# Attention on one core: sixteen lifted VectorE groups in halves, sixteen DMA turns, and another order

## The chip, the cores and the metric

The kernel runs on one core of a Trainium2 chip. The metric is device time in microseconds (us). The core has TensorE for matmuls, ScalarE for activations, VectorE and GpSimd for elementwise work, and DMA engines that move data. Each engine works through its own queue of instructions in order; semaphores tie the queues together. Data come from HBM into SBUF; matmuls write to PSUM, which ScalarE and VectorE read.

## The reference: what is computed

Attention for 8 batches of 8 heads, with 512 positions of 64 columns, all in float32:

```
scores = einsum('bhqd,bhkd->bhqk', q, k) / sqrt(64)
attn   = exp(scores - scores.max(-1)) ; attn /= attn.sum(-1)
out    = einsum('bhqk,bhkd->bhqd', attn, v)
```

Two heads are a pair, so there are 32 pairs, 0 to 31. The inputs are 25.2 MB, the output 8.4 MB.

## The kernel before: tiling, stages and the written order

For a pair, `q`, `k` and `v` are loaded as three tiles of 256 KB (`load`, line 183, on SyncE's queue) and cast to fp16 by GpSimd (`cast`, 191). `q` and `k` then have to lie with the 64 columns on the partitions. For most pairs TensorE transposes them into PSUM (`transposes`, 238) and VectorE copies the result out (`copy`, 257); for the pairs in `BY_DMA` one DMA does both (`turn`, 250), issued from SyncE's queue between loads and stores.

The scores are worked in groups: 128 keys of both heads of a pair against 512 queries, so 128 partitions by 1024 columns of float32 in PSUM (`scores`, 274). There are three such buffers, `st0` to `st2`. The step `S12.0` computes group 12 into buffer 0. Four groups make a pair; pair g has the groups 4g to 4g+3, and the last group of pair 31 is split into two halves of its queries (steps 127 and 128). No maximum is subtracted; the sum of the exponentials comes from a column of ones beside `v`.

For most groups ScalarE then computes the exponential into an fp16 tile `pt` (line 306). For 14 groups, listed in `KIND`, VectorE does it instead. For those of kind C, F and S a further matmul with the constant `lift` (line 287) first puts a large number under the scores, so that the float's low 16 bits hold the fraction of the exponent, and the columns of `k` of that group are multiplied by 128 log2(e) when cast (line 210). Then VectorE makes the fp16 bits with a polynomial: `r` (`raise_`, 323) writes `z`, and `p12.0` to `p12.2` (`pass_`, 338) are the passes on all 1024 columns. Kinds C and F have four VectorE passes; S and X have three, and a middle step `m` on GpSimd (`middle`, 371: a `tensor_scalar` and a product). X is not lifted. The last pass of the lifted kinds reads two tiles in SBUF, `y` and `z`, and writes 32-bit words to a tile `pd`; the fp16 halves of these are what the next matmul reads.

The values follow: `V1.0.2.14.0` is pair 1, head 0, query block 2, unit 14, in PSUM bank `x0` (`values`, 424: four matmuls). Seven units share a bank; `R` (`invert`, 393) takes the reciprocals of their sums, `N` (`normalise`, 398) multiplies into a ring in SBUF, and `O` (`store`, 412) stores the next pair whose units are done, or one head if its second number is 0. The last head's values are in `L` (`last_values`, 449, in a score buffer) and `F` (`finish`, 466). `B` (`fill`, 439) are matmuls on constants.

Nothing is planned at run time: `ORDER` is a literal list of steps, and each engine gets its instructions in the order of that list. `lk8` loads, `ck8` casts; `cv1+p5.2` casts only after that VectorE step has finished. TensorE, too, works strictly in this order, so a score that waits for its buffer holds everything behind it.

Of the kernel before, what the change touches and what calls it, by code (L numbers as in the profile page):

```python
# [19 lines left out]
RAW, QK16, TQK, NV = 7, 6, 7, 12  # L20
# [16 lines left out]
V3.1.3.35.1 V4.0.0.36.1 V4.0.1.37.1 cq11 lk15 S32.2 ck11+cq1 N28.7 lk16 S33.0 V4.0.2.38.1 p30.0
T9.0.0 lk17 cq12 V4.0.3.39.1 T9.1.0 S34.2 cv6 lq16 V4.1.0.40.1 C9 V4.1.1.41.1 cq13 S35.0 lv13 R35.7
p30.1 T10.0.0 T10.1.0 lq17 S36.2 lk18 C10 S37.1 cv5+p30.1 S38.0 N35.7 ck12 T11.0.0 lv12 T11.1.0
p30.2 S39.2 V4.1.2.42.1 V4.1.3.43.1 V5.0.0.44.1 S40.1 C11 cv7+p30.1 ck13 r39 S41.0 lv14 T12.0.0 cv8  # L40
lq18 T12.1.0 S42.1 lk19 cv10 C12 V5.0.1.45.1 lq19 V5.0.2.46.1 ck14 V5.0.3.47.1 p39.0 V5.1.0.48.1
O21.1 S43.0 V5.1.1.49.0 O35.1 V5.1.2.50.0 V5.1.3.51.0 V6.0.0.52.0 lv15 S44.1 R42.7 ck15 p39.1
V6.0.1.53.0 lk20 ck16 S45.0 cq14+r39 lk21 V6.0.2.54.0 N42.7 S46.2 V6.0.3.55.0 p39.2 lv17 T13.0.1
T13.1.1 S47.1 lk22 R49.7 S48.0 C13 cv9+R49.7 O42.1 S49.2 r47 cv12 V6.1.0.56.1 V6.1.1.57.1
V6.1.2.58.1 cq15 V6.1.3.59.1 S50.0 N49.7 lv16 V7.0.0.60.1 ck17 V7.0.1.61.1 V7.0.2.62.1 p47.0 S51.2
lq20 V7.0.3.63.0 cv11 V7.1.0.64.0 V7.1.1.65.0 lq21 V7.1.2.66.0 S52.0 cq16 R56.7 N56.7 V7.1.3.67.0
lq22 V8.0.0.68.0 ck18+N49.7 p47.1 S53.2 lq23 V8.0.1.69.0 T14.0.1 cq17 T14.1.1 lk23 S54.0 R63.7 C14
S55.1 cq18+R63.7 lv19 N63.7 S56.2 T15.0.1 O49.1 p47.2 T15.1.1 V8.0.2.70.0 V8.0.3.71.0 lk24
V8.1.0.72.0 S57.0 C15 lq24 S58.1 V8.1.1.73.0 r57 V8.1.2.74.0 ck19+C15 T16.0.1 lk25 T16.1.1 S59.2
cq19 lv18 V8.1.3.75.0 C16 V9.0.0.76.0 cq20 S60.1 O56.1 R70.7 ck20 V9.0.1.77.1 N70.7 lq25 S61.2 p57.0  # L50
V9.0.2.78.1 V9.0.3.79.1 O63.1 T17.0.0 cq21+p47.2 T17.1.0 S62.1 cv13+C1 lk26 C17 S63.0 V9.1.0.80.1
V9.1.1.81.1 p57.1 lk27 V9.1.2.82.1 S64.2 V9.1.3.83.1 lq26 V10.0.0.84.0 V10.0.1.85.0 V10.0.2.86.0
R77.7 cv15+C17 V10.0.3.87.0 V10.1.0.88.0 N77.7 V10.1.1.89.0 lq27 V10.1.2.90.0 ck21+p57.0 S65.0 R84.7
S66.1 N84.7 T18.0.1 lk28 S67.2 p57.2 lv20 V10.1.3.91.0 T18.1.1 V11.0.0.92.0 lv22 S68.0 C18
ck22+p57.2 lq28 r68 S69.1 cq22+C18 T19.0.1 lk29 V11.0.1.93.0 cq23 V11.0.2.94.0 S70.2 O70.1 p68.0
ck23 V11.0.3.95.0 T19.1.1 V11.1.0.96.0 cq24 V11.1.1.97.0 S71.1 R91.7 S72.0 m68.0 N91.7 S73.2 u22 C19
S74.1 r72 T20.0.1 V11.1.2.98.0 T20.1.1 u23 V11.1.3.99.0 S75.2 C20 V12.0.0.100.0 V12.0.1.101.0 p72.0
S76.1 lk30 cv14 V12.0.2.102.0 V12.0.3.103.0 V12.1.0.104.0 V12.1.1.105.1 ck24 S77.2 lv21 R98.7 p72.1
V12.1.2.106.1 lq29 ck25 S78.1 u24 V12.1.3.107.1 N98.7 cq25 V13.0.0.108.1 V13.0.1.109.1 S79.0 p68.2
V13.0.2.110.1 T21.0.0 u25 T21.1.0 V13.0.3.111.1 S80.1 C21 ck26 S81.2 S82.0 cq26+r5 R105.7 lq30 r81  # L60
V13.1.0.112.0 V13.1.1.113.0 O77.1 V13.1.2.114.0 cq27 V13.1.3.115.0 V14.0.0.116.0 S83.1 lq31 cv16
V14.0.1.117.0 N105.7 V14.0.2.118.0 cq28 lv23 S84.0 p81.0 V14.0.3.119.1 cv17 lk31 V14.1.0.120.1
V14.1.1.121.1 V14.1.2.122.1 S85.1 cv19 R112.7 V14.1.3.123.1 N112.7 V15.0.0.124.1 ck27 V15.0.1.125.1
S86.0 lv24 R119.7 p81.1 V15.0.2.126.0 lv26 V15.0.3.127.0 V15.1.0.128.0 ck28 V15.1.1.129.0
V15.1.2.130.0 S87.1 cv18 N119.7 V15.1.3.131.0 V16.0.0.132.0 S88.2 cv21+R119.7 lv25 R126.7
V16.0.1.133.1 N126.7 V16.0.2.134.1 cq29 O91.1 V16.0.3.135.1 V16.1.0.136.1 V16.1.1.137.1 S89.0 u26
p72.2 V16.1.2.138.1 V16.1.3.139.1 V17.0.0.140.0 V17.0.1.141.0 S90.2 V17.0.2.142.0 R133.7 ck29 O98.1
V17.0.3.143.0 N133.7 V17.1.0.144.0 S91.1 u27 p81.2 V17.1.1.145.0 S92.0 S93.2 V17.1.2.146.0
V17.1.3.147.1 r93 V18.0.0.148.1 cv20+p81.2 lv28 V18.0.1.149.1 V18.0.2.150.1 S94.1 O105.1 cq30
V18.0.3.151.1 V18.1.0.152.1 R140.7 V18.1.1.153.1 ck30 u28 N140.7 S95.0 S96.2 cv22 R147.7  # L70
V18.1.2.154.0 N147.7 V18.1.3.155.0 cv23 V19.0.0.156.0 V19.0.1.157.0 O112.1 V19.0.2.158.0
V19.0.3.159.0 p93.0 lv27 S97.0 V19.1.0.160.0 V19.1.1.161.1 V19.1.2.162.1 V19.1.3.163.1 R154.7
cv25+C2 V20.0.0.164.1 S98.2 N154.7 S99.1 m93.0 u29 S100.0 r99 V20.0.1.165.1 V20.0.2.166.1
V20.0.3.167.1 V20.1.0.168.0 V20.1.1.169.0 lv29 S101.2 V20.1.2.170.0 R161.7 O119.1 V20.1.3.171.0
N161.7 V21.0.0.172.0 V21.0.1.173.0 S102.0 u30 p99.0 V21.0.2.174.0 V21.0.3.175.1 V21.1.0.176.1
V21.1.1.177.1 V21.1.2.178.1 cv24+r99 S103.2 R168.7 V21.1.3.179.1 O126.1 cv26+R161.7 N168.7
V22.0.0.180.1 V22.0.1.181.1 S104.1 O133.1 R175.7 m99.0 S105.0 N175.7 V22.0.2.182.0 O147.1
V22.0.3.183.0 V22.1.0.184.0 O154.1 V22.1.1.185.0 V22.1.2.186.0 p93.2 V22.1.3.187.0 S106.2 O161.1
V25.0.0.188.0 O161.0 S107.1 V25.0.1.189.1 R182.7 V25.0.2.190.1 lv30 N182.7 S108.0 V25.0.3.191.1 r108
V25.1.0.192.1 V25.1.1.193.1 V25.1.2.194.1 S109.2 V25.1.3.195.1 V23.0.0.196.0 V23.0.1.197.0 R189.7  # L80
V23.0.2.198.0 S110.0 N189.7 cq31 S111.1 p99.2 S112.2 V23.0.3.199.0 V23.1.0.200.0 V23.1.1.201.0
V23.1.2.202.0 V23.1.3.203.1 V26.0.0.204.1 ck31+r5 R196.7 S113.0 r111 V26.0.1.205.1 cv27+C2 u31
S114.2 cv28 V26.0.2.206.1 N196.7 V26.0.3.207.1 V24.0.0.208.1 V24.0.1.209.1 S115.0 O168.0 R203.7
V24.0.2.210.0 p108.0 V24.0.3.211.0 O175.1 V24.1.0.212.0 S116.2 O182.1 V24.1.1.213.0 V24.1.2.214.0
N203.7 lv31 V24.1.3.215.0 m108.0 S117.0 p111.0 O189.1 V26.1.0.216.0 V26.1.1.217.1 O203.1
V26.1.2.218.1 V26.1.3.219.1 B220.1 B220.1 V28.0.0.220.1 S118.2 O203.0 R210.7 V28.0.1.221.1 N210.7
V28.0.2.222.1 S119.0 p111.1 V28.0.3.223.1 O210.1 V28.1.0.224.0 V28.1.1.225.0 V28.1.2.226.0
V28.1.3.227.0 B228.1 B228.1 S120.2 cv29 R217.7 B228.1 B228.1 B228.1 B228.1 N217.7 B228.1 B228.1
B228.1 B228.1 B228.1 B228.1 B228.1 B228.1 S121.0 p108.2 S122.1 O217.0 B228.1 B228.1 B228.1 B228.1
V29.0.0.228.0 V29.0.1.229.0 V29.0.2.230.0 V29.0.3.231.1 V29.1.0.232.1 R224.7 V29.1.1.233.1 p111.2  # L90
V29.1.2.234.1 V29.1.3.235.1 S123.2 S124.0 N224.7 cv30+p108.2 S125.1 V27.0.0.236.1 cv31+R224.7 O224.1
V27.0.1.237.1 V27.0.2.238.0 V27.0.3.239.0 R231.7 V27.1.0.240.0 V27.1.1.241.0 N231.7 V27.1.2.242.0
V27.1.3.243.0 V30.0.0.244.0 S126.2 O231.1 R238.7 N238.7 S127.0 V30.0.1.245.1 V30.0.2.246.1 O238.1
# [7 lines left out]
def kernel(  # L101
# [29 lines left out]
    for m, kind in KIND.items():  # L131
        (g, c, _), (g2, c2, _) = groups[m]
        assert 0 < g == g2 < LAST and c == c2
        if kind in LIFTED:
            raises.setdefault(g, set()).add(c)
# [138 lines left out]
    def scores(m, b):  # L274
# [33 lines left out]
        )  # L308

# [331 lines left out]
```

## Time and profile before

| | |
|---|---|
| median of three runs | 116.86 us (117.65, 116.73, 116.86) |
| span of the profiled execution | 114.0 us |
| TensorE, VectorE, ScalarE, GpSimd busy | 104.0, 103.2, 107.2, 81.7 us |
| loads and stores, all queues | 36.44 MB, mean 320 GB/s |

One execution was profiled. Its span runs from the first to the last instruction; its own device time is not listed apart from the three runs, so the median stands beside it. In the profile's rows PE is TensorE, PEld its weight loads, DVE VectorE, ACT ScalarE, POOL GpSimd, SP SyncE; a q behind the name is the queue that issues DMAs. L306 is line 306 of the kernel. A row of a group gives busy us, the mean ns of one, and after the bar the idle time just before its instructions with what ended it. A row of the timeline gives start, duration, engine, line and what was done. A duration contains the latency to the end of the instruction, so that one instruction can start before the one ahead is done.

### The profile page before, as it was taken

How to read it: one execution, taken by the hardware profiler on the slowest of the kernel's cores; microseconds unless marked ns; L12 is line 12 of the kernel's file. 1: busy time of each engine (PE TensorE's matmuls, PEld its weight loads, DVE VectorE, ACT ScalarE, POOL GpSimd, SP SyncE). 2: the span in 40 equal slices, each digit the busy share in tenths (PEclk: the TensorE clock that was granted, in tenths of full speed). 3: DMA queues.
4: the chain of work that ended last, by engine and by line, in shares of the span. 5: the costliest groups of instructions: out<-in, count | busy, mean ns of one | idle time of the engine just before them, and what ended most of it. 6: DMA issues, size and time to landing. Idle time of an engine off the chain costs nothing.

```text
span 114.0 us, 3954 instructions
## 1 busy us (share of the span) xinstructions
PE 104.0 (91%) x1549; PEld 65.6 (58%) x1549; DVE 103.2 (91%) x178; ACT 107.2 (94%) x119; POOL 81.7 (72%) x126
## 2 busy tenths in 40 slices
PE   7968998999899898999998899999999999999980
PEld 5624554655464564655665456775657666676660
DVE  4557999999999999999999999999989999999761
ACT  4599999999999999999999999999999999999960
POOL 2369756298978967938849999996899999394300
PEclk9999999999999999999999999999999999999999
DMA  3999999999999999999999998989999699999665
GB/s 92 281 354 378 383 378 384 382 380 378 383 384 376 385 382 381 375 368 382 376 385 384 369 196 283 188 209 383 279 257 232 219 333 328 312 312 330 226 218 164
DMA packets 45619, 36.44 MB, mean 320 GB/s; under 512 B 12704, under 2 KB 45600, under 8 KB 45600
## 3 DMA queue, kind: packets, MB, share of 16 engines
q1 hardware_dynamic: 45168, 35.86, 102.2%
q10 hardware_dynamic: 432, 0.33, 0.9%
q8 instruction: 12, 0.20, 0.7%
q14 instruction: 7, 0.06, 0.1%
HBM read 25.17 MB, written 8.39 MB: 294 GB/s over the span
## 4 chain that ended last, share of the span: by engine, by line
DVE 34%; PE 29%; ACT 23%; issue 5%; DMA 4%; POOL 1%; SPq 1%; ACTq 0%
ACT pt L306 23%; PE o L431 14%; PE st L301 13%; DVE y L361 12%; DVE tqk L266 6%; DVE z L328 5%; DVE ring L404 4%; DVE pd L361 4%; DMA k<-in_k_dram 4%; DVE rc L396 1%; PE tp L246 1%; PE o L441 1%; SPq L486 1%; DVE tqk L260 1%; PE st L287 1%
## 5 line engine op out<-in xcount | busy, mean ns | idle before, releaser
L306 ACT ACTIVATE pt<-st 128x1024 f16<-128x1024 f32 (+1 forms) x112 | 102.3, 1097 | 0.4 <-PE st L301 0.4
L301 PE MATMUL st<-tqk 64*128 64x512 f16 (+1 forms) x250 | 46.7, 380 | 5.3 <-ACT pt L306 3.5
L431 PE MATMUL o<-vp,pt 128*128 128x65 f16 x912 | 45.4, 195 | 0.0
L431 PEld LDWEIGHTS <-pt 128*128 128x128 f16 x912 | 36.2, 98 | 14.5 <-issue 13.3
L195 POOL CAST vp<-v 128x512 f16<-128x512 f32 x32 | 24.1, 768 | 8.5 <-DVE pd L361 2.8
L301 PEld LDWEIGHTS <-tqk 64*128 64x128 f16 x250 | 14.2, 93 | 17.9 <-issue 7.8
L404 DVE TENSOR_TENSOR ring<-o,rc 128x448 f32<-128x448 f32 (+2 forms) x37 | 22.5, 608 | 1.0 <-DVE rc L396 0.2
L220 POOL CAST qkp<-k 128x512 f16<-128x512 f32 (+3 forms) x27 | 18.0, 672 | 4.7 <-issue 2.4
L220 POOL CAST qkp<-q 128x512 f16<-128x512 f32 x30 | 18.1, 611 | 1.6 <-DVE y L361 0.8
L328 DVE TENSOR_SCALAR z<-st 128x1024 f32<-128x1024 f32 x14 | 17.0, 1211 | 1.4 <-PE st L301 1.3
L361 DVE SCALAR_TENSOR_TENSOR pd<-y,z 128x1024 uint32<-128x1024 f32 x12 | 15.3, 1272 | 0.0
L431 PE MATMUL o<-vp,pd 128*128 128x65 f16 x96 | 15.1, 195 | 0.0
L246 PE MATMUL tp<-ident,qkp 128*128 128x128 f16 x168 | 14.6, 220 | 0.4 <-POOL qkp L220 0.2
L361 DVE SCALAR_TENSOR_TENSOR y<-st,z 128x1024 f32<-128x1024 uint16 x12 | 14.6, 1213 | 0.0
L266 DVE COPY tqk<-tp 128x1024 f16<-128x1024 f16 x20 | 13.6, 682 | 0.1
L246 PEld LDWEIGHTS <-qkp 128*128 128x128 f16 x168 | 9.8, 97 | 4.5 <-issue 1.6
L431 PEld LDWEIGHTS <-pd 128*128 128x128 f16 x96 | 9.4, 98 | 2.7 <-issue 2.2
L361 DVE SCALAR_TENSOR_TENSOR y<-st,y 128x1024 f32<-128x1024 uint16 x9 | 10.9, 1209 | 0.0
L396 DVE RECIPROCAL rc<-o 128x7 f32<-128x7 f32 (+2 forms) x37 | 7.2, 195 | 1.3 <-PE o L431 1.3
L208 POOL CAST qkp<-k 128x384 f16<-128x384 f32 (+2 forms) x8 | 3.3, 412 | 4.8 <-DVE pd L361 3.3
L210 POOL TENSOR_SCALAR qkp<-k 128x128 f16<-128x128 f32 x12 | 6.3, 527 | 0.2
L376 POOL TENSOR_SCALAR t<-y 128x1024 f32<-128x1024 f32 x4 | 4.2, 1045 | 2.4 <-DVE y L361 2.1
(58 smaller groups left out, 52.1 us busy)
## 6 DMA issues: line engine op xcount, KB each, us to landing
v<-in_v_dram SPq DMA_DIRECT2D x32, 256.0 KB, 5.4
k<-in_k_dram SPq DMA_DIRECT2D x31, 256.0 KB, 5.4
q<-in_q_dram SPq DMA_DIRECT2D x31, 256.0 KB, 5.4
out_dram<-ring SPq DMA_DIRECT2D x29, 256.0 KB, 4.8
out_dram<-ring SPq DMA_DIRECT2D x5, 128.0 KB, 3.1
k<-in_k_dram ACTq DMA_DIRECT2D x2, 128.0 KB, 2.8
q<-in_q_dram SPq DMA_DIRECT2D x2, 128.0 KB, 2.6
tqk<-qkp SPq DMA_TRANSPOSE x10, 5.3
```

The costliest lines, as they stand in the source:

```text
L195: return nc.gpsimd.tensor_copy(out=vps[g % NV][:, :, :, 0:D], in_=raw[g]["v"][:, :, :, :])
L210: nc.gpsimd.tensor_scalar(out=dst[:, :, c : c + 1], in0=src[:, :, c : c + 1], scalar1=128.0 * LOG2E, scalar2=None, op0=AluOp.mult,)
L220: parts.append(nc.gpsimd.tensor_copy(out=dst[:, :, a:NI], in_=src[:, :, a:NI]))
L246: nc.tensor.transpose(tps[g][:, n, i, :], qkp[g][:, n, i, :], ident)
L266: nc.vector.tensor_copy(out=tqk[g][:, :, :], in_=tps.pop(g).rearrange("p n i c -> p n (i c)"))
L301: nc.tensor.matmul(st[:, x, cols], kc, qc[:, cols], start=kind is None or kind not in LIFTED, stop=True)
L306: nc.scalar.activation(out=pt[:, :, cols], in_=st[:, :, cols], func=EXP, scale=scale)
L328: nc.vector.tensor_scalar(out=r["z"][:, :, :], in0=r["st"][:, :, :], scalar1=2.0**17 if lifted else 128.0 * LOG2E, scalar2=None if lifted ...
L361: nc.vector.scalar_tensor_tensor(out=r["bits"][:, :, :] if last else y, in0=(zero, one, y)[s], scalar=(QUARTIC if quartic else CUBIC)[s], ...
L396: dve(nc.vector.reciprocal(out=rcs[u][:, 0:n], in_=o[:, x : x + n, D : D + 1]))
L404: nc.vector.tensor_tensor(out=ring[:, u % NU : u % NU + n, :], in0=o[:, x : x + n, 0:D], in1=rc[:, 0:n].broadcast_to([P, n, D]), op=AluOp. ...
L431: nc.tensor.matmul(os[u // 7][:, u % 7, :], blocks[(g, c, h)][:, y * P : (y + 1) * P], vps[g % NV][:, h, c, :], start=(c == 0), stop=(c == ...
```

## The change

16 groups instead of 14 go to VectorE, all of one kind. Each is lifted, and `k` of the 15 pairs that have such a group is scaled as a whole when cast, in one `tensor_scalar` with two operations (the second a product with 1); ScalarE's scale undoes it for the pair's other groups. The polynomial is written as a product: VectorE forms (x + a) times a constant (`r`), then (x + b) times that (`p..0`), GpSimd squares the result (`m`), and VectorE adds score and square (`p..2`) and writes fp16 bits straight to a `pt` tile. Each of these is done in halves of 512 columns, one head each; `r5.1` is the half of head 1. `pd` goes, and `pt` has 40 buffers instead of 30. The pairs 16 to 31, instead of 22 to 31, are turned by DMA. The order is another one in whole: groups are no longer in sequence, the lifted groups always use buffer 2, and no cast waits for a VectorE step any more.

```diff
-KIND = {5: "C", 12: "C", 20: "C", 30: "C", 39: "C", 47: "C", 57: "F", 68: "S", 72: "C", 81: "C", 93: "X", 99: "S", 108: "X", 111: "C"}
-BY_DMA = (22, 23, 24, 25, 26, 27, 28, 29, 30, 31)
+BY_VECTOR = (5, 12, 21, 28, 31, 46, 53, 59, 69, 72, 79, 91, 94, 107, 111, 115)
+BY_DMA = (16, 17, 18, 19, 20, 21, 22, 23, 24, 25, 26, 27, 28, 29, 30, 31)
...
+        if name == "k" and g in scaled:
+            return nc.gpsimd.tensor_scalar(
+                out=dst,
+                in0=src[:, :, :, :],
+                scalar1=to_bits,
+                scalar2=1.0,
+                op0=AluOp.mult,
+                op1=AluOp.mult,
+            )
...
+            scale=scale / to_bits if grp[0][0] in scaled else scale,
```

The steps `r`, `p` and `m` of the changed kernel, whole:

```python
    def raise_(m, h):
        r = raised[m]
        if "t" not in r:
            r["t"] = wpool.tile([P, 2, S], FP32, tag="z", name=f"t_{m}")
        dve(
            nc.vector.tensor_scalar(
                out=r["t"][:, h],
                in0=fraction(r["st"])[:, h],
                scalar1=ROOTS[0],
                scalar2=Q2**0.5,
                op0=AluOp.add,
                op1=AluOp.mult,
            )
        )

    def pass_(m, s, h):
        r = raised[m]
        t = r["t"][:, h]
        if s == 0:
            dve(
                nc.vector.scalar_tensor_tensor(
                    out=t,
                    in0=fraction(r["st"])[:, h],
                    scalar=ROOTS[1],
                    in1=t,
                    op0=AluOp.add,
                    op1=AluOp.mult,
                )
            )
            return
        dve(
            nc.vector.scalar_tensor_tensor(
                out=r["bits"][:, h],
                in0=r["st"][:, h],
                scalar=BOTTOM,
                in1=r["y"][:, h],
                op0=AluOp.add,
                op1=AluOp.add,
            )
        )

    def square(m, h, engine):
        r = raised[m]
        if "y" not in r:
            r["y"] = wpool.tile([P, 2, S], FP32, tag="y", name=f"y_{m}")
        t = r["t"][:, h]
        return engine.tensor_tensor(out=r["y"][:, h], in0=t, in1=t, op=AluOp.mult)

    def middle(m, h):
        square(m, h, nc.gpsimd)
```

Two stretches of the new order that the prediction speaks of, a turn up to its pair's first score, and the end:

```
S78.1 V13.0.1.109.1 cq25 V13.0.2.110.1 r79.0 V13.0.3.111.1 V13.1.0.112.0 cq24 S70.0 lv19 p79.0.0
V13.1.1.113.0 V13.1.2.114.0 cv14 u24 S76.1 R105.7 V13.1.3.115.0 N105.7 cq29 V14.0.0.116.0
V14.0.1.117.0 V14.0.2.118.0 p79.0.1 m79.0 S88.0 V14.0.3.119.1 V14.1.0.120.1 R112.7 lk31 S85.1 N112.7
m79.1 V14.1.1.121.1 O63.1 V14.1.2.122.1 p79.2.0 V14.1.3.123.1 V15.0.0.124.1 lv21 V15.0.1.125.1 S87.0
R119.7 ck29 O35.1 p79.2.1 V15.0.2.126.0 O7.1 S77.1 N119.7 S91.2 u25 V15.0.3.127.0 r91.1 S99.0
...
V29.1.0.232.0 V29.1.1.233.0 V29.1.2.234.0 R224.7 S127.0 S128.2 N224.7 V29.1.3.235.0 cv31
V27.0.0.236.0 V27.0.1.237.0 S121.1 R231.7 cv30 V27.0.2.238.1 L0.0 L1.0 V27.0.3.239.1 L2.2 F0
V27.1.0.240.1 V27.1.1.241.1 L3.2 N231.7 V27.1.2.242.1 V27.1.3.243.1 S124.1 F1 O224.1 V30.0.0.244.1
V30.0.1.245.0 V30.0.2.246.0 O238.1 R238.7 V30.0.3.247.0 V30.1.0.248.0 N238.7 V30.1.1.249.0
V30.1.2.250.0 V30.1.3.251.0 O245.1 R245.7 V31.0.0.252.1 V31.0.1.253.1 N245.7 V31.0.2.254.1
V31.0.3.255.1 R252.4 O231.1 N252.4 O252.0
```

More of the change, by code (lines that the diff above doesn't have):

```diff
@@ L90 @@
[L90 to L93, printed above, removed]
-V30.0.3.247.1 V30.1.0.248.1 V30.1.1.249.1 V30.1.2.250.1 V30.1.3.251.1 V31.0.0.252.0 V31.0.1.253.0
-R245.7 V31.0.2.254.0 V31.0.3.255.0 N245.7 S128.2 L0.0 R252.4 L1.0 O245.1 L2.1 N252.4 O252.0 F0 L3.1
@@ L327, in raise_ @@
         dve(
             nc.vector.tensor_scalar(
-                out=r["z"][:, :, :],
-                in0=r["st"][:, :, :],
-                scalar1=2.0**17 if lifted else 128.0 * LOG2E,
-                scalar2=None if lifted else 143.0 * 1024,
-                op0=AluOp.max if lifted else AluOp.mult,
-                **({} if lifted else {"op1": AluOp.add}),
-            )
-        )
-    def pass_(m, s):
-        r, kind = raised[m], KIND[m]
-        if kind in ("X", "Q") and s == 2:
+                out=r["t"][:, h],
```

245 lines of the change are left out of this document (98 added, 147 removed).

## The prediction

> **What bounds the kernel now.** First the page's engine totals, then the groups by shape.
>
> ```profile
> span 114.0 us, 3954 instructions
> PE 104.0 (91%) x1549; PEld 65.6 (58%) x1549; DVE 103.2 (91%) x178; ACT 107.2 (94%) x119; POOL 81.7 (72%) x126
> ...
> L306 ACT ACTIVATE pt<-st 128x1024 f16<-128x1024 f32 x110 | 101.2, 1106 | 0.1
> ```
>
> Three engines stand above 90%, so totals don't decide. The group does: the 110 exponentials of full size on ScalarE waited 0.1 us in all, and 101.2/110 = 0.92 us is the step from one to the next. The timeline of ScalarE's two ends says the same:
>
> ```profile
> 7.81 6.73 ACT L306 ACTIVATE pt<-st 128x1024 f16<-128x1024 f32 x7
> ...
> 102.53 7.06 ACT L306 ACTIVATE pt<-st 128x1024 f16<-128x1024 f32 x8
> 109.97 0.60 ACT L306 ACTIVATE pt<-st 128x512 f16<-128x512 f32 x1 [0.37 <-PE st L301]
> ```
>
> It runs from 7.81 to 109.59 without a gap (110 x 0.92 and one half of about 0.5 make 101.7). **ScalarE is the bound.** VectorE, GpSimd and TensorE matter only if late. What follows the last exponential is the tail; timeline of TensorE, VectorE and the two issuing queues:
>
> ```profile
> 108.03 1.58 PE L431 MATMUL o<-vp,pt 128*128 128x65 f16 x44
> 109.54 0.39 PE L301 MATMUL st<-tqk 64*128 64x256 f16 x2
> ...
> 110.62 0.30 PE L457 MATMUL o_last<-vp,pt 128*128 128x65 f16 x4 [0.21 <-ACT pt L306]
> ...
> 109.92 0.17 DVE L396 RECIPROCAL rc<-o 128x4 f32<-128x4 f32 x1
> 110.13 0.42 DVE L404 TENSOR_TENSOR ring<-o,rc 128x256 f32<-128x256 f32 x1
> ...
> 110.58 0.34 SPq L422 DMA_DIRECT2D out_dram<-ring  x1
> 111.02 0.40 SPq L479 DMA_DIRECT2D out_dram<-obl  x1
> ...
> 111.48 0.35 ACTq L479 DMA_DIRECT2D out_dram<-obl  x1
> ...
> out_dram<-ring SPq DMA_DIRECT2D x5, 128.0 KB, 3.1
> ...
> out_dram<-obl SPq DMA_DIRECT2D x1, 64.0 KB, 2.0
> out_dram<-obl ACTq DMA_DIRECT2D x1, 64.0 KB, 1.7
> ```
>
> The last store (64 KB, issued at 111.48) lands 1.7 later, at 113.2; 0.8 us closes the span at 114.0. The tail after the last exponential (110.57) is 3.4 us. The span stands against runs of 116.73 to 117.65 (median 116.86): 2.9 us lie around it, and I carry them over.
>
> **ScalarE.** 16 lifted groups instead of 14 leave 108 full exponentials: 2 x 0.92 = **-1.84 us**, where every step stays dense. The changed scale factor of some costs nothing: same instruction, same size.
>
> **VectorE.** Its timeline:
>
> ```profile
> 19.55 0.68 DVE L266 COPY tqk<-tp 128x1024 f16<-128x1024 f16 x1
> 20.15 0.61 DVE L404 TENSOR_TENSOR ring<-o,rc 128x448 f32<-128x448 f32 x1
> 20.68 1.22 DVE L361 SCALAR_TENSOR_TENSOR pd<-y,z 128x1024 uint32<-128x1024 f32 x1
> 21.82 0.68 DVE L266 COPY tqk<-tp 128x1024 f16<-128x1024 f16 x1
> ```
>
> Start to start, 1024 columns cost 1.14 and 448 cost 0.53; the line through both gives 0.60 at 512, of which 0.06 is fixed. Out go 14 `r` and 38 `p` steps, 52 x 1.14 = 59.3; in come 16 groups x 3 passes x 2 halves, 96 x 0.60 = 57.6. Six pairs fewer are copied from PSUM (0.60 each, 19.55 to 20.15): -3.6. Sum -5.3 us, and it buys only slack, since ScalarE ends last. [...]
>
> **GpSimd.** Its timeline, then groups by shape.
>
> ```profile
> 5.99 0.29 POOL L208 CAST qkp<-k 128x128 f16<-128x128 f32 x1 [1.47 <-DMA k<-in_k_dram]
> ...
> 85.90 1.89 POOL L379 TENSOR_TENSOR y<-t 128x1024 f32<-128x1024 f32 x1
> 87.74 1.17 POOL L195 CAST vp<-v 128x512 f16<-128x512 f32 x2
> ...
> 62.97 1.04 POOL L376 TENSOR_SCALAR t<-y 128x1024 f32<-128x1024 f32 x1
> 64.10 2.36 POOL L379 TENSOR_TENSOR y<-t,y 128x1024 f32<-128x1024 f32 x1
> ...
> L220 POOL CAST qkp<-q 128x512 f16<-128x512 f32 x30 | 18.1, 611 | 1.6 <-DVE y L361 0.8 <-DVE rc L396 0.5 <-DMA q<-in_q_dram 0.3
> L210 POOL TENSOR_SCALAR qkp<-k 128x128 f16<-128x128 f32 x12 | 6.3, 527 | 0.2
> L208 POOL CAST qkp<-k 128x128 f16<-128x128 f32 x3 | 0.9, 292 | 1.5 <-DMA k<-in_k_dram 1.5
> ```
>
> A square of 1024 takes 1.84 start to start; a half lies between 0.92 and, with the casts' fixed 0.19, 1.04: I take 1.0, so 32 halves add 32 us, and four middle steps go (1.04 with 1.89 or 2.36, some 13 in all). Casts follow 0.56 us apart (two take 1.17). Fifteen `k` tiles are now scaled whole, a form not in the trace (512 columns, two operations, fp16 out). From below it is the plain cast, 0.61; from above it is the 128-column scaling, 0.527, stretched by four less its fixed part: (0.527 - 0.19) x 4 + 0.19 = 1.54. The two-operation row (1024 columns in 1.04) lies on the casts' line (0.19 + 0.83 per 1000 columns), so I take 0.61. Counted so along the order, GpSimd has 12 squares and 44 casts = 36.6 us ahead of the 48th score step, from its first cast at 5.99 to 42.6; ScalarE by then has 41 exponentials, 7.81 + 37.7 = 45.5. So GpSimd leads by **2.9 us** at most. About half goes at the start, when loads and the first square's input aren't there yet; 1.5 us is the slack I use. The passes with two SBUF inputs (`pd<-y,z`) are gone: each new pass reads one operand in PSUM. The waits that put casts behind those passes go too. I cost that at nothing gained, since ScalarE never waited for it. [...]
>
> **TensorE.** Chain of waits:
>
> ```profile
> 54.84 0.45 PE tp L246 x8
> ...
> 84.88 0.22 PE st L287 x2
> ```
>
> Six pairs of transposes go, 12 steps `T` of four matmuls each (eight in 0.45: -2.7). 16 groups are lifted where 12 were (the two of kind X had no lift): 4 x 0.22 = +0.9. Fill matmuls stay at 44. TensorE only has to stay ahead; nothing is gained from it.
>
> **DMA and its queue.** Six more pairs are turned by DMA. View of the tile `tqk`, then half-microsecond windows around one turn:
>
> ```profile
> L252 SPq DMA_TRANSPOSE tqk<-qkp x10: 1237/1720/3149, 62.0 to 97.7; - x10
> ...
> DMA to landing us min/median/max: 3.7/5.3/6.2
> ...
> 81.00:81.50 0.50, 0.50 (x13) 0.35 (x12) 0.50 (x2) 0.50 (x2) 0.50 (x2) 1.00 1.16 403
> 81.50:82.00 0.50, 0.50 (x11) 0.20 (x7) 0.47 (x2) 0.50 (x2) 0.50 (x2) 1.00 4.13 252
> 82.00:82.50 0.50, 0.50 (x12) 0.27 (x9) 0.47 (x3) 0.50 (x2) 0.50 (x2) 1.00 0.03 3
> ```
>
> A turn's 256 KB pass in about 0.9 us (126 KB in the second window, the rest in the first), so six cost the engines some 5 us, and hold the queue 6 x 1.2 to 3.1 us with loads and stores behind. Loads are issued at least five steps ahead of their casts, which hides it; without that cover six turns at the median 1.7 would cost 10 us. The latency has less: the order puts `u31`, the tightest before, 9.2 us of exponentials ahead of its pair's first score; now `u24` and `u26` stand five steps (4.6 us) ahead, five others seven. I cost this at zero in the forecast and keep it as a rival.
>
> **The tail, worked out.** The changed order ends `S127.0 S128.2 S121.1 ... S124.1`, then eight `V30`, four `V31.0`, `R252 N252 O252`. The two halves now lie inside the dense stretch, but S121 and S124 share buffer 1, so S124's matmul waits for S121's exponential. S121 ends at 109.59 - 3 x 0.92 + 0.49 (S128's half, no longer behind) = 107.3; the matmul ends at 107.8; the exponential (1106 ns) at 108.9; 16 `V31.0` matmuls (0.16 + 16 x 0.032) at 109.6; reciprocal to issue takes 0.66 as at 109.92 to 110.58: issue at 110.3. This store is 128 KB, between the 64 KB row (1.7) and the 128 KB row (3.1, most of them under load); before, the one issued at 110.58 stood ahead of a store that landed at 113.0, so 2.4 bounds it if they land in turn. I take 2.3: 112.6, and 0.8 closes at 113.4. So of 1.84 us the longer tail eats 1.2: **-0.6 us, 116.3 us**, with 115.6 to 117.1 from the two landing rows.
>
> **The rivals.** *The tail costs no more than now* and the gain shows whole: 116.86 - 1.84 = 115.0. For it: the changed tail's last bytes are few, and small stores landed in 1.7. Against: the last block's division and a larger store stand behind the last full exponential.
>
> *Transposes late.* TensorE fills a buffer one step ahead, so `u24` and `u26` have 3.7 us; landing takes 3.7, 5.3 or 6.2. At the median each is late by 1.6 us, the second perhaps not if the first has pushed everything back: 117.9, or 119.5 with both. For it: the landing row; against: the queue may issue ahead of its place in the order. It decides where a turn lands over 3.7 us after issue.
>
> *GpSimd becomes the bound early (slower).* Nine scaled casts and 12 squares lie ahead of the 48th step. At 1.54 a cast they cost 9 x 0.93 = 8.4 us more, less the slack of 1.5: +6.9, 123.2; half-way between the ends (1.08) it is +2.7, 119.0. VectorE's last pass waits for the square, the lifted group keeps its buffer, and TensorE stands in front of the next lifted score. It decides from about 0.78 us a cast (1.5/9 over 0.61), or a half square over 1.12. For it: 0.527 for 128 columns; against: the two-operation row. In this case the change doesn't do what it says, as ScalarE waits longer than the two exponentials it lost.
>
> **How the numbers follow.** Forecast 116.3 (115.6 to 117.1) 0.43; short tail 0.18; late transposes 0.22; GpSimd 0.12; 0.05 for anything else slow. One per cent, 1.17 us, is about what can be told from no change here: faster is below 115.7 (the short tail and a little of the forecast: 0.21), slower above 118.0 (half the late transposes, GpSimd, the rest: 0.29), within 0.50. The range, 114.9 to 119.8, takes in the short tail and both late turns, and the lower half of the GpSimd case; its upper half stays out.
>
> **What would show it.** ScalarE with 108 full exponentials at 0.92 and no idle to speak of before S121, then one gap near 0.5 us: right. Idle before exponentials released by a score that waited for `tqk` written by DMA: late transposes. A scaled cast near 1.5, or half squares over 1.1, and VectorE waiting for `y`: GpSimd. [...] The last store landing 3 us after issue would move the end to 114.2.

## The result, and the profile after

The changed kernel takes **126.31 us** (median of four runs, 124.53 to 127.81) against 116.82 before, where I forecast 0.6 us less. Some executions here and below were disturbed ones, longer at a lower granted clock, so each time that follows is the median of the others (with the range of all in brackets), ratios leave them out, and an asterisk marks numbers from the profile of one. So taken the changed kernel has 124.69 us, **7.9 us longer** than before, a ratio of 1.066 (1.060 to 1.071). The profiled execution took 124.85 us, with a span of 123.1.

First the page of the changed kernel: totals, DMA row of the 40 slices, DMA queue, then the groups that answer to those shown of before.

```profile
span 123.1 us, 3858 instructions
...
PE 103.8 (84%) x1509; PEld 64.6 (53%) x1509; DVE 100.2 (81%) x216; ACT 106.8 (87%) x117; POOL 88.5 (72%) x134
...
DMA  4999999999999899999999999969999989999675
...
q1 hardware_dynamic: 51504, 37.43, 104.1%
...
L296 ACT ACTIVATE pt<-st 128x1024 f16<-128x1024 f32 (+1 forms) x110 | 101.9, 1051 | 8.4 <-PE st L291 7.8
...
L358 POOL TENSOR_TENSOR y<-t 128x512 f32<-128x512 f32 x32 | 33.0, 1040 | 7.5 <-DVE t L332 6.8
...
L206 POOL TENSOR_SCALAR qkp<-k 128x512 f16<-128x512 f32 x15 | 9.3, 617 | 4.3 <-DMA k<-in_k_dram 3.1
```

No engine has become busier than ScalarE, and ScalarE is no longer dense: its exponentials waited 8.4 us for scores, where they had waited 0.1, or 0.4 with the two halves (x110 are 108 whole ones and two halves). The timeline of ScalarE has each gap in brackets, with what ended it:

```profile
8.21 1.06 ACT L296 ACTIVATE pt<-st 128x1024 f16<-128x1024 f32 x1
9.60 1.02 ACT L296 ACTIVATE pt<-st 128x1024 f16<-128x1024 f32 x1 [0.33 <-PE st L291]
10.87 9.31 ACT L296 ACTIVATE pt<-st 128x1024 f16<-128x1024 f32 x10 [0.24 <-PE st L291]
20.43 23.07 ACT L296 ACTIVATE pt<-st 128x1024 f16<-128x1024 f32 x25 [0.26 <-PE st L291]
43.69 22.50 ACT L296 ACTIVATE pt<-st 128x1024 f16<-128x1024 f32 x24 [0.19 <-PE st L291]
67.83 12.14 ACT L296 ACTIVATE pt<-st 128x1024 f16<-128x1024 f32 x13 [1.63 <-PE st L291]
82.49 18.58 ACT L296 ACTIVATE pt<-st 128x1024 f16<-128x1024 f32 x20 [2.52 <-PE st L291]
...
117.49 1.02 ACT L296 ACTIVATE pt<-st 128x1024 f16<-128x1024 f32 x1 [2.46 <-PE st L291]
```

The span is thereby accounted for. Before, it was 7.81 of start, 102.76 from the first of these exponentials to the end of the last, and 3.4 of tail; now it is 8.21, 110.30 (117.49 + 1.02 less 8.21) and 4.6. Of the middle's +7.5 us, 7.9 are gaps (8.4 against the 0.37 before the last half and 0.1). The two exponentials fewer, worth 1.84, show as only 0.4: the exponential ahead of a gap costs its full 1.02 to 1.06 (the rows of a single one), not the 0.92 from start to start, and there are some ten gaps.

What TensorE waited for ahead of the three long gaps, from its timeline:

```profile
67.34 0.39 PE L291 MATMUL st<-tqk 64*128 64x512 f16 x2 [1.58 <-DMA tqk<-qkp]
...
80.00 0.39 PE L277 MATMUL st<-const-bfloat16-1.0,lift 64*128 64x512 bf16 x2 [1.45 <-DVE pt L343]
82.00 0.39 PE L291 MATMUL st<-tqk 64*128 64x512 f16 x2 [1.16 <-DMA tqk<-qkp]
...
115.62 0.41 PE L434 MATMUL o_last<-vp,pt 128*128 128x65 f16 x8 [1.43 <-POOL vp L195]
```

The first is pair 20's turn. Its last cast started at 57.38, but `u20` was issued at 62.39: SyncE's queue, in order and without a pause, was still at `u19`, `lv17`, `lv13`, `lv12`, `lq23` and `lk30`. Timelines of GpSimd and of that queue:

```profile
57.38 0.61 POOL L214 CAST qkp<-k 128x512 f16<-128x512 f32 x1
```

```profile
56.95 1.60 SPq L245 DMA_TRANSPOSE tqk<-qkp  x1
58.60 1.70 SPq L189 DMA_DIRECT2D v<-in_v_dram  x3
60.34 0.47 SPq L189 DMA_DIRECT2D q<-in_q_dram  x1
60.86 1.44 SPq L189 DMA_DIRECT2D k<-in_k_dram  x1
62.39 1.30 SPq L245 DMA_TRANSPOSE tqk<-qkp  x1
```

The second gap is that of a lifted group whose square was late, and then `u24`. The third is `cv31`, whose load had been issued at 109.64 behind stores. Each looks like a mishap of its own. The chain of waits, of before and of after, says what they share:

```profile
DVE 34%; PE 29%; ACT 23%; issue 5%; DMA 4%; POOL 1%; SPq 1%; ACTq 0%
```

```profile
DMA 41%; ACT 22%; DVE 15%; PE 9%; POOL 5%; issue 4%; SPq 1%; ACTq 0%; POOLq 0%
```

### The profile page after: what moved, and what is told of

Read it like the earlier page. It is cut to its first block, busy times and chain, and to the rows that moved or that the text cites. A ratio compares the mean times of both kernels' runs of the same rounds, so it can differ in the third digit from the quotient of the medians.

```text
span 123.1 us, 3858 instructions
## 1 busy us (share of the span) xinstructions
PE 103.8 (84%) x1509; PEld 64.6 (53%) x1509; DVE 100.2 (81%) x216; ACT 106.8 (87%) x117; POOL 88.5 (72%) x134
## 3 DMA queue, kind: packets, MB, share of 16 engines
q1 hardware_dynamic: 51504, 37.43, 104.1%
## 4 chain that ended last, share of the span: by engine, by line
DMA 41%; ACT 22%; DVE 15%; PE 9%; POOL 5%; issue 4%; SPq 1%; ACTq 0%; POOLq 0%
ACT pt L296 22%; DMA tqk<-qkp 18%; DMA v<-in_v_dram 11%; DMA q<-in_q_dram 5%; DMA k<-in_k_dram 4%; PE st L291 4%; DVE ring L377 4%; DVE t L317 4%; DMA out_dram<-ring 3%; DVE pt L343 3%; PE o L403 3%; DVE t L332 3%; PE tp L239 2%; POOL y L358 2%; POOL vp L195 1%
## 5 line engine op out<-in xcount | busy, mean ns | idle before, releaser
L358 POOL TENSOR_TENSOR y<-t 128x512 f32<-128x512 f32 x32 | 33.0, 1040 | 7.5 <-DVE t L332 6.8
L343 DVE SCALAR_TENSOR_TENSOR pt<-st,y 128x512 uint16<-128x512 f32 x32 | 21.6, 683 | 3.8 <-POOL y L358 3.7
L195 POOL CAST vp<-v 128x512 f16<-128x512 f32 x32 | 19.2, 615 | 7.2 <-DMA v<-in_v_dram 6.9
L317 DVE TENSOR_SCALAR t<-st 128x512 f32<-128x512 uint16 x32 | 21.2, 681 | 2.2 <-PE st L291 1.7
L332 DVE SCALAR_TENSOR_TENSOR t<-st,t 128x512 f32<-128x512 uint16 x32 | 21.5, 681 | 0.4
L206 POOL TENSOR_SCALAR qkp<-k 128x512 f16<-128x512 f32 x15 | 9.3, 617 | 4.3 <-DMA k<-in_k_dram 3.1
L259 DVE COPY tqk<-tp 128x1024 f16<-128x1024 f16 x14 | 9.5, 680 | 2.0 <-PE tp L239 2.0
L214 POOL CAST qkp<-k 128x512 f16<-128x512 f32 x16 | 9.8, 612 | 1.8 <-PE st L291 1.3
L277 PE MATMUL st<-const-bfloat16-1.0,lift 64*128 64x512 bf16 x32 | 6.2, 379 | 2.2 <-DVE pt L343 1.8
L418 PE MATMUL o<-const-bfloat16-1.0 128*128 128x65 bf16 x44 | 5.4, 196 | 0.0
```

Of the source, the lines that this page charges most:

```text
L195: return nc.gpsimd.tensor_copy(out=vps[g % NV][:, :, :, 0:D], in_=raw[g]["v"][:, :, :, :])
L214: return nc.gpsimd.tensor_copy(out=dst, in_=src[:, :, :, :])
L259: nc.vector.tensor_copy(out=tqk[g][:, :, :], in_=tps.pop(g).rearrange("p n i c -> p n (i c)"))
L317: nc.vector.tensor_scalar(out=r["t"][:, h], in0=fraction(r["st"])[:, h], scalar1=ROOTS[0], scalar2=Q2**0.5, op0=AluOp.add, op1=AluOp.mult,)
L332: nc.vector.scalar_tensor_tensor(out=t, in0=fraction(r["st"])[:, h], scalar=ROOTS[1], in1=t, op0=AluOp.add, op1=AluOp.mult,)
L343: nc.vector.scalar_tensor_tensor(out=r["bits"][:, h], in0=r["st"][:, h], scalar=BOTTOM, in1=r["y"][:, h], op0=AluOp.add, op1=AluOp.add,)
```

## The experiments

### Each late thing by itself, in the changed order

Four kernels, each with one edit of the changed one: TensorE takes pairs 16 to 21 back; the square becomes a copy; `qkp` has 9 buffers; `lv31` stands earlier.

```diff
- u16 ... u21
+ T16.0.x T16.1.x C16 ... (one of the two banks, between units)
```


> The changed kernel with the pairs 16 to 21 transposed on TensorE again (steps T and C in place of u), all else as changed. Theory 'turns': six more turns in SyncE's queue make the queue and the landings late; then the idle of ScalarE before scores of pairs 20 and 24 (1.63 and 2.52 us) goes, and the time falls by 4 us or more, to 120.5 or less against 124.7 for the changed kernel. Theory 'GpSimd': the turns are late because the casts ahead of them are; then TensorE's transposes wait for the same casts, and the time stays over 123. The six copies add 3.6 us to VectorE and 2.7 us to TensorE, which both have room.

```diff
-        return engine.tensor_tensor(out=r["y"][:, h], in0=t, in1=t, op=AluOp.mult)
+        return engine.tensor_copy(out=r["y"][:, h], in_=t)
```


> The changed kernel with a plain copy in place of GpSimd's square (the square is left out, so the lifted groups' exponentials are not the reference's). A copy of 512 columns should take 0.61 us as the casts do, not 1.04: 32 x 0.43 = 13.8 us less on GpSimd, all waits and the order the same. Theory 'GpSimd': GpSimd is full from 10 to 75 us, and its lateness makes casts and turns late; the time falls to 121 or less, and the idle before pairs 20 and 24 goes. Theory 'turns': the time stays within 1 us of the changed kernel (124.7).

```diff
-RAW, QK16, TQK, NV, NP16 = 7, 6, 7, 12, 40
+RAW, QK16, TQK, NV, NP16 = 7, 9, 7, 12, 37
```


> The changed kernel with 9 buffers for the fp16 q and k (qkp) instead of 6, and 37 pt buffers instead of 40 to make room. Theory 'buffers': a cast waits for the landing of an earlier turn (76.6 us in the changed kernel's profile, 1.94 us idle on GpSimd), the square behind it and the next turn come late by that, and the idle of 2.52 us of ScalarE at 80 us goes: 122 or less. Theories 'turns' and 'GpSimd' without that link: no change beyond 0.7 us (124 to 125.4).

```diff
-... lv30 ... lv31
+... lv30 lv31 ...
```


> The changed kernel with the load of the last v tile moved ahead of the stores in SyncE's queue, right behind the load of v of pair 30. If that load's place behind stores is what holds TensorE before the last score (2.46 us of idle on ScalarE at 115 us, of which 0.5 belong to the shared buffer), the time falls by 1.5 to 2.5 us, to 122.2 to 123.2. If the queue as a whole is late, something else is late next there and it falls by less than 0.8.

| kernel | us (runs) | ratio to before |
|---|---|---|
| TensorE turns 16 to 21 | 131.30 (130.18 to 134.19) | 1.124 (1.114 to 1.134) |
| copy for square | 125.98 (125.83 to 128.19) | 1.088 (1.074 to 1.102) |
| 9 `qkp` buffers | 126.39 (126.18 to 131.51) | 1.086 (1.077 to 1.095) |
| `lv31` early | 124.48 (124.11 to 126.00) | 1.071 (1.060 to 1.082) |

None gives anything back that these runs could tell, against 124.69 and 1.066 as changed; each theory of a single cause had asked for 1.5 us or more. With the copy, ScalarE has no gap of note from 12.6 to 65.9, but 2.6 us at 68.5 and 1.7 at 82.8. With nine buffers the gap at 82 is gone, the one at 67.9 stays (2.0), and others stand at 73.2 (1.0) and 95.9 (1.3). With `lv31` early the last gap falls from 2.46 to 0.87 and the others stay. Take one lateness away and the next appears, which suggests that something they share is short. The first kernel is worse by 6.6 us and says little of the turns, as I had to put the transposes 0.9 to 3.7 us ahead of their scores, into TensorE's strict order.

### Turns in the order of before

Five kernels that keep the order of before, so that nothing of the VectorE part is in. In the first, pairs 16 to 21 are turned by DMA too:

```diff
-... T16.0.1 ... T16.1.1 ... C16 ...
+... cq16 ... u16 ...      (two score steps behind the casts; 16 to 21)
```


> The kernel before, its order kept, but with pairs 16 to 21 turned by DMA as well: their transposes and copies are taken out, and each turn stands two score steps behind its casts, 7.4 to 13.8 us of exponentials ahead of its pair's first score. Nothing of the VectorE part is in. 'Short leads' (sixteen turns cost nothing where they stand early enough): within 1 us of before, 115.5 to 118. 'Sixteen turns are too many' (SyncE's queue or the DMA engines are full, whatever the order): six times the median issue of 1.7 us that is no longer hidden, 119 or more, with casts waiting for loads.

The second moves the ten turns of before close to their scores:

```diff
-S73.2 u22 C19 S74.1 ...
+... u22 S83.1 ...      (five score steps ahead of the first score; 22 to 31)
```


> The kernel before, with its ten turns (pairs 22 to 31) moved so that each stands 4.6 us of exponentials ahead of its pair's first score, where u24 and u26 stand in the changed order; all else as before. 'Short leads': a landing of 5.3 us against 3.7 to 4.6 makes most of them late by 0.7 to 1.6 us; a turn that was pushed back gives the next one more room, so not all pay: 119.5 to 126, ScalarE idle before scores that waited for tqk from DMA. 'Sixteen turns are too many': ten turns are as before, 116 to 118.

The third adds three turns instead of six (`u17`, `u19`, `u21`):

> The kernel before, with pairs 17, 19 and 21 alone turned by DMA in addition, two score steps behind their casts, 10.1 to 12.9 us ahead. 'DMA engines full': each turn adds 1.9 us of packets to engines that have little room, so half the price of six more (125.7 against 116.6): 119 to 122.5. 'Places of the turns' (u16 and others stood badly, not their number): 118 or less.

The fourth has no turns:

```diff
-                kc = tqk[g][s, 1, c * P : (c + 1) * P]
+                kc = tqk[13 if g in BY_DMA else g][s, 1, c * P : (c + 1) * P]
```


> The kernel before without its ten turns: scores of pairs 22 to 31 read the transposes of pair 13 (so those scores are left out of the result), 29 pt buffers instead of 30. The kernel before has ScalarE without gaps while the DMA engines are 0.9 busy or more in nearly all slices. 'ScalarE bounds it, with the DMA engines just short of full': 115.5 to 117.5, no change, DMA idle at the end. 'It was bound by the DMA engines already': below 115.

The fifth has sixteen turns and smaller loads of `v`:

```diff
-            nc.sync.dma_start(out=t[:, :, :, :], in_=source(src, g))
+            n = 1 if name == "v" and g > 15 else NI
+            nc.sync.dma_start(out=t[:, :, 0:n, :], in_=source(src, g)[:, :, 0:n, :])
```


> The kernel before with sixteen turns at long leads (the run that took 125.7), and with the loads of v for pairs 16 to 31 issued at their places but bringing a quarter of their bytes, read by nobody (the casts of these pairs read pair 15's tile, so those values are left out of the result; 29 pt buffers instead of 30). Every issue of SyncE's queue stays, and the order is that of before. 'DMA engines full': quarter loads took 7 us of packets away in the changed kernel, which is 3 to 4 turns, so 118.5 to 121.5. 'SyncE's queue full' (the number and kind of issues counts): 123.5 or more.

"Packets" is the DMA queue's row of each page, share times span: the time that the packets of the one large queue took, summed over 16 engines and divided by 16. It can pass the span (104.1% in the changed kernel), so packets overlap. "Issues" is the sum of the durations in the timeline of SyncE's queue.

| order of before | us (runs) | packets, us | issues, us | ratio |
|---|---|---|---|---|
| no turns | 116.84 (116.08 to 119.62) | 98.0 | 77.9 | 1.002 (0.997 to 1.006) |
| ten turns (before) | 116.82 | 116.5 | 89.5 | 1 |
| thirteen turns | 119.82 (119.80 to 123.08) | 123.6* | 99.1* | 1.028 (1.017 to 1.039) |
| sixteen turns | 125.59 (124.38 to 126.59) | 128.5 | 100.6 | 1.080 (1.071 to 1.090) |
| sixteen turns, quarter loads | 120.96 (120.54 to 122.95) | 120.8* | 100.7* | 1.038 (1.029 to 1.046) |
| ten turns, close to their scores | 122.20 (121.75 to 125.95) | 118.6* | 89.3* | 1.048 (1.036 to 1.059) |

**Six more turns cost 9 us in the old order too**, 7.4 to 13.8 us ahead of their scores, with no VectorE change. That is more than the whole change cost (7.9). From none to ten, turns are free (116.84 and 116.82); beyond ten, six cost 1.5 us each ((125.59 - 116.57)/6), three 1.0 each ((119.82 - 116.69)/3, with the kernel before at 116.57 and 116.69 beside them). The rows behind "packets", of the pages of before, of before without turns, and of before with sixteen:

```profile
DMA  3999999999999999999999998989999699999665
...
q1 hardware_dynamic: 45168, 35.86, 102.2%
```

```profile
DMA  3999999999999999999999939678989783151572
...
q1 hardware_dynamic: 34608, 33.24, 85.0%
```

```profile
DMA  3999999999999999999999989999997999999994
...
q1 hardware_dynamic: 51504, 37.43, 104.8%
```

Each digit is the busy share of the 16 DMA engines in a fortieth of the span. In before they are at 0.9 or more almost to the end: by this row the **DMA engines were full beside ScalarE**. Without the ten turns they have pauses from the 24th slice on, and the time doesn't change: there ScalarE alone bounds it, as I had said. By the packets, ten turns take (116.5 - 98.0)/10 = 1.85 us of all 16 engines each; a load of the same 256 KB takes 98.0 x 0.262/33.24 = 0.77.

The quarter loads leave the issues where they are (100.7 us) and give back 4.7 of the 9 us; at 120.96 that is inside the range of 'DMA engines full' and 2.5 below that of 'SyncE's queue full'. So what the transfers take counts by itself, with one reserve: no cast of `v` waits for these loads any more, which alone was worth 1.0 us in the changed order (below) and was not run alone in this one. How much of the rest is the queue's stays open: both sums grow by 11 to 12 us with six turns, and the trace of before has turn issues of 1.24 to 3.15 us, so that a queue that stops at full engines would look the same.

Where the sixteen turns of the old order hurt is seen in the waits of that run (sum in us, times, longest):

```profile
POOL qkp L219 <- DMA tqk<-qkp: 6.6, 2, 5.3
PE st L300 <- DMA tqk<-qkp: 3.0, 1, 3.0
```

GpSimd stood 5.3 us before a cast whose `qkp` buffer a turn still had, and TensorE 3.0 us before a score whose turn hadn't landed. Whether more `qkp` buffers would have helped there was not run; nine of them did not help the changed kernel.

Turns close to their scores cost 5.6 us by themselves, without one turn more. TensorE waited 3.4 us* for one turn in this run, and GpSimd 5.6 us* in all for `qkp` buffers that a turn still had.

### The DMA work in the changed order

Now the same in the changed kernel. Turns that nobody reads, six turns out (two choices, and with the copy), all out, and `v` loads out, cut to quarters or unread. The edits are of one kind:

```diff
-                kc = tqk[g][s, 1, c * P : (c + 1) * P]
+                kc = tqk[14 if g in BORROW else g][s, 1, c * P : (c + 1) * P]
...
-                in_=raw[g]["v"][:, :, :, :]
+                in_=raw[min(g, 15)]["v"][:, :, :, :]
```


> The changed kernel with all sixteen turns issued and landing as they are, but the scores of pairs 16 to 31 read the transposes of pair 14 instead (so the scores of those pairs are left out of the result), and 39 pt buffers instead of 40. No score waits for a turn. 'Late turns': the gaps of 1.6 and 2.5 us at 67.8 and 82.5 go, the one for v31 stays: 119.5 to 123, ScalarE idle 2 to 4.5 us. 'Load on the queue' (loads and casts are late behind the turns, whether their scores wait or not): 124 or more.

> The changed kernel without the turns of pairs 16 to 21: their scores read the transposes of pair 14 instead (so those scores are left out of the result), 39 pt buffers; the ten other turns stand where they stand, 4.6 to 9.2 us ahead. 'DMA engines full': the queue's packets took 104.1% of 123.1 us in the changed kernel and 102.2% of 114.0 us in the kernel before, 11.6 us more, so 1.9 us a turn; with six turns fewer the work is that of before, and the time comes to 115 to 118.5. 'Short leads' (late order of the ten that stay): 121 or more.

> The same with all sixteen turns left out (scores of pairs 16 to 31 read pair 14's transposes; those scores are left out of the result). 'DMA engines full': with 31 us of packets gone no load is late, ScalarE is dense and the time is the one that I worked out for a dense ScalarE, 114 to 117. If GpSimd, VectorE or the order itself holds ScalarE up, idle of more than 3 us stays and the time is 118 or more.

> The changed kernel with all its sixteen turns, but without the loads of v for pairs 16 to 31: their casts read the raw tile of pair 15 (so those values are left out of the result). 16 x 256 KB at the 380 GB/s of a slice without turns are 11 us of DMA, about as much as six turns. 'DMA engines full' (any transfer left out helps alike): 115 to 118.5. 'Turns late by themselves' (a turn's latency or its place in the queue): 121 or more, with the gaps before scores that wait for tqk still there.

> The changed kernel without the turns of pairs 16 to 21 (their scores read pair 14's transposes, those scores are left out of the result) and with a copy in place of GpSimd's square (the polynomial is left out of the result). In the run with the six turns out alone, SyncE's queue stood at 56.7 to 59.9 and 67.0 to 70.3 before a turn whose cast was not done, with the DMA engines 0.7 to 0.8 busy, and the ten turns and the last loads crowded the last 35 us. 'GpSimd late holds the queue': casts come sooner, the queue doesn't stand, 115.5 to 119. 'The order crowds the ten turns in any case': 120.5 or more.

> The changed kernel without the turns of pairs 26 to 31 (their scores read pair 14's transposes, those scores are left out of the result); the turns of pairs 16 to 25 stay, ten as in the kernel before. 'Sum of DMA work, and where it lies': as many turns as with pairs 16 to 21 out, but the last 40 us have four fewer: 116.5 to 120, below the 121.3 to 125.3 of that run. 'Only the sum counts': the same 121 to 125 as that run.

> The changed kernel with all turns and all loads issued at their places, but the loads of v for pairs 16 to 31 bring only a quarter of their bytes (one of four rows of each partition, in pieces of 256 bytes) and are read by nobody: the casts of these pairs read pair 15's tile (so those values are left out of the result); 39 pt buffers. 'DMA engines full': less to move, so near the 118.9 of the run without these loads, 118 to 121. 'SyncE's queue full' (the number of issues counts, not what they move): no better than with whole unread loads, 122 or more.

> The same with whole loads of v for pairs 16 to 31, landing unread. DMA work is that of the changed kernel; only no cast of v waits for them. 'DMA engines full': the turns are as late as in the changed kernel, the last gap of 2.5 us goes: 122 to 125.5. 'Late v casts' (what healed the run without these loads was that no cast waited): 118 to 120.5.

| changed order | us (runs) | packets, us | issues, us | ScalarE's idle, us |
|---|---|---|---|---|
| all turns out | 118.75 (118.36 to 119.67) | 98.4 | 83.3 | 2.2 |
| sixteen `v` loads out | 118.89 (118.16 to 120.32) | 116.4* | 92.9* | 2.5* |
| turns 26 to 31 out | 123.70 (122.98 to 125.42) | 117.0* | 95.6* | 8.4* |
| turns 16 to 21 out, copy for square | 122.50 (122.04 to 123.90) | 118.6 | 88.2 | 4.9 |
| turns 16 to 21 out | 121.33, one run (to 125.27) | 119.2* | 93.6* | 6.7* |
| quarter `v` loads, unread | 122.05 (121.38 to 128.07) | 121.3* | 100.5* | 9.6* |
| as changed | 124.69 (124.53 to 127.81) | 128.1 | 100.1 | 8.4 |
| turns unread | 126.76 (126.08 to 128.94) | 128.6 | 102.5 | 10.3 |
| whole `v` loads, unread | 123.65, one run (to 127.34) | 129.8* | 102.6* | 8.2* |

The first lesson is that of the turns unread: **no score waits for a turn, and not a microsecond comes back.** The late turns that the profile names are where the shortage shows, not what it is. TensorE's 3.5 us of waits for turns are gone, but ScalarE's idle is 10.3 us instead of 8.4, and its last gap 4.15 instead of 2.46; GpSimd waits for loads of `v` as long as before (7.0 us against 6.9). The page of this run, slices and groups:

```profile
PE   7878889888998988899979959699999999995870
...
PEclk9999999999999999999999995557999999999687
DMA  3899999999999999999999999999999999999174
...
L195 POOL CAST vp<-v 128x512 f16<-128x512 f32 x32 | 19.2, 615 | 7.4 <-DMA v<-in_v_dram 7.0
```

The granted clock (row `PEclk`) fell to 0.5 for three slices in this run, so some of what came back may have been lost there again; that wasn't separated.

The second is that of the two runs at the top: with all turns out, or with sixteen `v` loads out and every turn in place, ScalarE's idle falls to 2.2 and 2.5 us and the rest of the change is seen: 118.8. (Both times lie above what I had given for 'DMA engines full', by 1.8 and 0.4 us.) That it is the work of those loads, transfer and issue, and not the wait for them, the whole unread loads show: no cast waits, and the one time of 123.65 is 1.0 below the changed kernel's, not 5.8. The page with all turns out, totals and group of the exponentials:

```profile
span 116.3 us, 3835 instructions
...
q1 hardware_dynamic: 34608, 33.24, 84.6%
...
L297 ACT ACTIVATE pt<-st 128x1024 f16<-128x1024 f32 (+1 forms) x110 | 101.2, 1060 | 2.2 <-PE st L292 2.0
```

So even with DMA to spare the changed kernel is not faster than before (1.021, 1.011 to 1.031).

Against my expectation, six turns fewer don't bring it there, whichever six. They give back 3.4 us (one run) and 1.0 of 5.9. With 16 to 21 out, ScalarE has no gap over 0.26 us from 9 to 86 us* and then 5.9 us of them; with 26 to 31 out, 6.0 us of gaps lie between 65 and 87*, and after that only 0.87. The lateness goes where turns are out and stays where ten are left, although their sums are near those of before. What those ten have less of is lead: with 16 to 21 out 4.6 to 9.2 us instead of 9.2 to 15.6, with 26 to 31 out the same for nine of the ten; and ten turns at 4.6 us cost 5.6 us in the old order, too. That the lead is the cause here is argued from this, as no run gave these ten more of it. GpSimd's squares aren't it: with the copy besides, the time is 122.50, no less than without and still far from 118.8.

The loads of `v` tell a little more of the queue. Without them `u20` is issued at 59.52* instead of 62.39; with quarter loads, whose issues stay, at 62.29*. Queue of the kernel without them, then of that with quarters:

```profile
59.52 1.25 SPq L244 DMA_TRANSPOSE tqk<-qkp  x1
```

```profile
62.29 1.24 SPq L247 DMA_TRANSPOSE tqk<-qkp  x1
```

At that place it is the queue's work, not the bytes, that makes `u20` late. So both are short, the engines and the queue that feeds them. The quarter loads' runs spread so widely (121.4 to 128.1) that I take no share from them; how the 5.9 us between all turns and none divide wasn't settled.

### The VectorE part alone

The 14 lifted groups of before in halves, with squares on GpSimd, in the order of before:

```diff
-r12 ... p12.0 ... p12.1 ... p12.2
+r12.1 r12.0 ... p12.0.1 m12.1 p12.0.0 m12.0 ... (three score steps) p12.2.1 p12.2.0
```


> The VectorE and GpSimd part alone in the order of before: its 14 lifted groups worked in halves, three passes and a square on GpSimd, k scaled as a whole, all of them lifted, no cast behind a VectorE pass; ten turns, 110 full exponentials. A lifted group keeps its score buffer three score steps past its second pass, and where that meets the old buffer numbers the two others take turns. 'The order is to blame': 115.5 to 118.5, ScalarE idle under 2 us. 'The VectorE part is to blame' (squares late, buffers held): 119 or more, with TensorE waiting for VectorE and VectorE for the square.

134.56 us, one run (to 139.59). This is a price of my order and no verdict on the halves: a lifted group now needs its score buffer until its last pass, and GpSimd, strictly in order, stood before squares for 29.6 us*, with casts behind it.

```profile
POOL y L359 <- DVE t L333: 29.6, 12, 8.6
```

So placed, this VectorE part doesn't fit the old order; what it costs in a better one is suggested by the changed kernel without turns: ScalarE's idle there is 2.2 us in all.

## Why the prediction was wrong

**ScalarE as the bound of before:** right. Without any turn the time is the same (1.002), and ScalarE has no gap but the 0.37 before its last half.

**The step that failed** is in the part on DMA: "Loads are issued at least five steps ahead of their casts, which hides it; without that cover six turns at the median 1.7 would cost 10 us", costed at zero. The cover wasn't there: six more turns cost 9.0 us in the old order, and without any turn the changed kernel is 5.9 us shorter. That the 10 us that I set aside lie near is luck, since they were six times the queue's time for an issue and not a price of what the engines do. In the changed order six turns fewer gave back only 1.0 to 3.4 us; the ten that stay cost 2.6 to 5.0 more than none, and the short leads, which the same paragraph also costed at zero, are the likely part of that. Two readings went wrong. First, I counted busy engines among the compute engines and never read the DMA row: a lead of five steps hides a delay, but not more work for engines that are 0.9 busy in nearly every slice; there the delay adds up (3.1 us for three turns more in the old order, 9.0 for six), and SyncE's queue is late, too (`u20` 4.4 us behind the end of its last cast). Second, the size. I took 0.9 us for a turn from the bytes that passed. The windows of before that I quoted have the DMA share just ahead of the rate, and one of them reads 4.13: half a microsecond in which packets began that take 2.07 us of 16 engines. The windows that follow:

```profile
82.50:83.00 0.50, 0.50 (x22) 0.50 (x18) 0.50 (x2) 0.50 (x1) 0.50 (x2) 1.00 0.08 9
83.00:83.50 0.50, 0.26 (x8) 0.22 (x4) 0.50 (x1) 0.50 (x2) 0.50 (x2) 1.00 0.71 153
83.50:84.00 0.50, 0.50 (x10) 0.27 (x10) 0.50 (x1) 0.50 (x1) 0.50 (x1) 1.00 1.20 358
```

From 82.0 to 83.0 the engines moved 3 and 9 GB/s. I count that quiet to the turn, whose packets began just ahead: over 81 to 84 the six windows average 196 GB/s against 383 from 80.5 to 81. The queue's rows say the same by another way: 1.85 us for a turn against 0.77 for a load of the same bytes.

**The rival "transposes late"** named `u24`, and `u24` is in the trace (1.16 us of TensorE, after 1.45 for a late square); `u26` isn't, and pair 20's turn is. But its mechanism, the landing of single turns, isn't the price in the changed order: unread turns cost as much. Short leads do cost in the old order: 1.048 for ten turns at 4.6 us, 5.6 us, where this rival had 1.6 to 3.2.

**GpSimd's prices** came out as picked: half square 1.04 (1.0), whole scaled cast 0.617 (0.61). So the rival "GpSimd bound early" stayed small: the four gaps up to 44 us make 1.0 us, and with a copy for the square ScalarE is dense from 12.6 to 65.9.

Of the two `y<-t,y` rows of before, of which the prediction shows one (2.36), the other took 3.34, so the four middle steps that went were 13.7 us by their rows, where I had some 13.

**VectorE:** a half pass after a half pass costs 0.60, as drawn from the line through two rows; in the timeline of VectorE two together take

```profile
29.68 1.28 DVE L332 SCALAR_TENSOR_TENSOR t<-st,t 128x512 f32<-128x512 uint16 x2
```

that is 0.68 for the second and 0.60 for the step. It was slack, and remained so.

**The tail:** worked out as 4.5 us from the end of the last exponential, measured 4.6. But the gap ahead of that exponential, put at 0.5, was 2.46, since `cv31` came late; with `lv31` early it is 0.87.

**Beyond DMA**, 2.4 us lie between the forecast (116.3) and the run without turns (118.75): its idle is 2.2 where I had 0.5, and its tail 5.2 (last exponential from 110.06 to 111.08, span 116.3).

## What to carry to other kernels

Read the DMA row of the 40 slices with the same care as the engines' totals: where it stands at 0.9 throughout, and the issuing queue has no pauses, one more transfer can have a price however early it stands (here six turns, 7.4 to 13.8 us ahead, cost 9.0 us); a lead hides latency, not work. Price a transfer by the engine time of its packets (the queue's share times the span, or the share in a window), not by its bytes: a turn took 1.85 us, 2.4 times the 0.77 of a load of the same size. When a wait in the trace is to be blamed, take away the wait and keep the work; if the time stays, look for what the waits share.

## What I had not expected of the hardware

- By its packets a DMA transpose of 256 KB within SBUF took 1.85 us of all 16 DMA engines, 256 KB loaded or stored 0.77; around one transpose they moved under 10 GB/s for 1 us.
- In one and the same order turns were free up to a point and cost 1.0 to 1.5 us each beyond it: 0 and 10 turns 116.8 us, 13 turns 119.8, 16 turns 125.6.
- The granted clock fell in some runs near gaps in which ScalarE waited for TensorE's scores. With sixteen turns in the order of before ScalarE had a gap of 2.78 us up to 80.1 (TensorE waited 3.0 us for one turn in that run), and the clock over 73 to 83 and 83 to 93 us was 0.79 and 0.87. With turns unread it was 0.5 in three slices in a row, from 75.0 us on, after a gap of 1.24 us that ended at 75.1; the changed kernel's profile, with gaps of 1.63 and 2.52 us, has 1.00 up to 113 us. So the length of one gap doesn't settle it. Whether a late transfer thereby costs a second time wasn't measured; if it does, that is in the 9.0 us above.
